# Mixer constants and gate rows loaded from GpSimd's queue, paired copies, and a split last product bank in a decoder layer

## The chip, the cores and the metric

The kernel runs on one core of a Trainium2 chip. The metric is the time of one execution in device microseconds. A core has five engines with instruction streams of their own, each of which runs its stream in order: TensorE (PE; the loading of its weights is listed apart as PEld), VectorE (DVE), ScalarE (ACT), GpSimd (POOL) and SyncE (SP). An engine that issues a transfer does so in its own stream; such issues are listed as SPq, ACTq or POOLq. Sixteen DMA engines carry the transfers of all queues.

## The reference

A decoder layer over 256 rows of width 1024: a half-weighted SwiGLU block, a token mixer, a second SwiGLU block, and a final RMSNorm. Each block is normalised, shifted, scaled and gated by vectors worked out from a conditioning row c.

```python
mod = (silu(c) @ w_ada + b_ada)                      # nine vectors of 1024
n = rmsnorm(h, g_ffn1) * (1 + sc1) + sh1
h = h + 0.5 * gt1 * ((silu(n @ w1_gate) * (n @ w1_up)) @ w1_down)
n = rmsnorm(h, g_mix) * (1 + sc2) + sh2
u, q, k, v = split(n @ w_in)                         # 512 columns each
y_pool = per group g of 4: ((mean over the last 2/4/8/16 rows) - u) @ w_pool[g] * pool_scale
y_attn = 8 heads of 64: three dilated causal windows with distance penalties, merged by their sums
h = h + gt2 * (concat(y_pool, y_attn) @ w_out)
n = rmsnorm(h, g_ffn2) * (1 + sc3) + sh3
h = h + 0.5 * gt3 * ((silu(n @ w2_gate) * (n @ w2_up)) @ w2_down)
out = rmsnorm(h, g_final)
```

The inner width of the SwiGLU blocks is 2816, cut into 11 chunks of 256. The three dilated windows are folded into one table of penalties (`bias`), 256 columns for each head, and the trailing means into band matrices (`band`), one for each of the four groups.

## The kernel before

The 256 rows are two tiles of 128, t = 0 and 1. All weights come through one sequence of units (`plan`), 1 MB each, which SyncE loads into four buffers `raw`. A unit of weights is split on the chip into a high part (`hi`, a cast on ScalarE, L288) and a low part (`lo`, a subtraction on VectorE, L289), and each product is done as three: hi by hi, low of the activations by hi, hi by low of the weights. A unit of the modulation (`ada`) is instead reduced on VectorE (L277). The order of the work within an engine is set by the Tile layer's scheduler, from the order of the code and from priorities (`urgent`).

`norm_rows` closes a block for one tile: gate (L330), add to h (L332), the sum of squares in two halves of 512 columns (L334), the power -0.5 on GpSimd (L337), and the scaled rows `xs` (L339 on ScalarE, L340 on VectorE). `norm_mod` turns them by TensorE (L316; `xt`, as `xtb` ahead of the mixer and `xtc` behind it) and applies shift and scale. The turns of tile 0 stand among the products of tile 1 of the same block (`accf`, `accm`), and those of tile 1 among the first products of the next block (`zp`, `le`).

In the mixer, `zchunk` makes the products `zp` and copies them to `z`; the turned `q` and `k` (`tq`, `tk`) come from it. `scores` multiplies them for a pair of heads, adds a bias table and exponentiates, `heads_out` turns the probabilities (`pt` to `pts`) and multiplies with v (`yt`), and `pool_group` does the band product (`po`) and the group's map (`pw`). Both write the mixer's output `y` as high and low part. All the constants of the mixer, the gate rows (`gate_rows`: through a small buffer `gd` in DRAM, then spread over 128 partitions into `gt`) and `gfb` are loaded from ScalarE's stream.

A load takes one of a few semaphores in turn, and so waits for the load that used it before. The loads of SyncE and ScalarE share one set of them (`DMAHW`); those of GpSimd have another (`DMASW`).

`finish3` ends the kernel: gate, add, sum of squares, scaling by the power and by `gfb`, and the store, in column parts. Ahead of it the last four chunks of tile 1 are multiplied for columns 0 to 511 first (`banks` (0,)), and then for 512 to 1023.

Of the kernel before, what the change touches and what calls it, by code (L numbers as in the profile page):

```python
# [10 lines left out]
F32 = mybir.dt.float32  # L11
# [4 lines left out]
P = 128  # L16
S = 256
# [28 lines left out]
SPIN = (4, 8, 8, 5)  # L46
PARTS = 11
# [123 lines left out]
def block_kernel(ctx, tc, w, vec, x, c, gf, wpool, bandd, biasd, out):  # L171
# [153 lines left out]
    def norm_rows(t, tag, accs, g, units):  # L325

        ss = None
        for b in range(2):
            tmp = work.tile([P, 512], F32, name=f"res{tag}{b}", tag="t2", bufs=T2)
            nc.vector.tensor_tensor(tmp, accs[b], g[:, ts(b, 512)], ALU.mult)  # L330
            hs = h[:, t * D + b * 512:t * D + b * 512 + 512]
            nc.vector.tensor_tensor(hs, hs, tmp, ALU.add)  # L332
            v = tiny.tile([P, 1], F32, name=f"v{tag}{b}", tag="v")
            nc.vector.tensor_tensor_reduce(tmp, hs, hs, 1.0, D * EPS if ss is None else ss, ALU.mult, ALU.add, v)  # L334
            ss = v
        r = tiny.tile([P, 1], F32, name=f"r{tag}", tag="r")
        nc.gpsimd.tensor_tensor(r, ss, mhalf, ALU.pow)  # L337
        xs = [work.tile([P, 512], F32, name=f"xs{tag}{b}", tag="t2", bufs=T2) for b in range(2)]
        rows = [nc.scalar.activation(xs[0], h[:, t * D:t * D + 512], AF.Copy, scale=r),  # L339
                nc.vector.tensor_scalar(xs[1], h[:, t * D + 512:t * D + D], r, None, ALU.mult)]  # L340
# [31 lines left out]
    def gate_rows(gtm, factor):  # L372
# [7 lines left out]
        nc.scalar.dma_start(d, sb)  # L380
        g = work.tile([P, D], F32, name=f"gt{gtm}", tag="gt", bufs=1)
        nc.scalar.dma_start(g, d.rearrange("(o a) b -> o (a b)", o=1).to_broadcast([P, D]))
# [38 lines left out]
    def down(f, ci, t, hid, accs, banks=(0, 1)):  # L421
        hi, lo = want("down", (f, ci))
        hh, hl = hid
        for k in range(2):
            first, last = ci == 0 and k == 0, ci == NCH - 1 and k == 1
            for (a, ww, st, sp) in ((hh, hi, first, False), (hl, hi, False, False), (hh, lo, False, last)):
                for b in banks:
                    mm(accs[b], a[:, k, :], cols(ww, 2 * k + b), start=st, stop=sp)  # L428

# [40 lines left out]
    def ffn_rest(f, ci0, n, prev, pci, accs, finish, gate):  # L470
# [19 lines left out]
        for banks in ((0, 1),) if f == 0 else ((0,), (1,)):  # L490
            for ci in last:
                if after and ci == last[TURN]:
                    after()
                down(f, ci, 1, hid[ci][1], accs[1], banks)
# [170 lines left out]
    probs = {}  # L665

    def scores(hp):
# [6 lines left out]
        both = xp.tile([P, 2 * S], F32, name=f"bias{hp}", tag="bias", bufs=3)  # L674
        nc.scalar.dma_start(both, biasd[:, 2 * hp * S:2 * hp * S + 2 * S])
        for e in range(2):
            hd = 2 * hp + e
            with urgent():
                ps, bias = pss[e], both[:, ts(e, S)]
# [4 lines left out]
                for t, sl in ((0, slice(0, P)), (1, slice(P, 3 * P))):  # L684
                    nc.vector.tensor_tensor_reduce(p[:, sl], ps[:, sl], bias[:, P:S] if t == 0 else bias, 1.0, 3e38,
# [8 lines left out]
    def heads_out(hp, v, y):  # L694
# [13 lines left out]
        with urgent():  # L708
            for t in range(NT):
                split(y[t][0][:, 4 + hp, :], y[t][1][:, 4 + hp, :], ps[:, ts(t, P)])  # L710

    def pool_group(g, u, y):
        bands = xp.tile([P, 2 * P + 16], F32, name=f"bands{g}", tag="bands", bufs=4)
        nc.scalar.dma_start(bands, bandd[:, g])
        wp = xp.tile([P, P], F32, name=f"wp{g}", tag="wp", bufs=4)
        nc.scalar.dma_start(wp, wpool[:, ts(g, P)])
# [101 lines left out]
    nc.scalar.dma_start(gfb, gf.to_broadcast([P, D]))  # L818
    nc.scalar.mul(gfb, gfb, float(D) ** 0.5)

    def finish3(t):
        with urgent():
# [3 lines left out]
            for part in (((0, 512),), ((512, 768), (768, D))):  # L826
                acc_b = nm["acc"][t][part[0][0] // 512]
                for a, b in part:
                    nc.vector.tensor_tensor(o[:, a:b], acc_b[:, a % 512:(b - 1) % 512 + 1], g[:, a:b], ALU.mult)
                for a, b in part:  # L830
                    nc.vector.tensor_tensor(ht[:, a:b], ht[:, a:b], o[:, a:b], ALU.add)
                for a, b in part:
                    sq = work.tile([P, 512], F32, name=f"sqo{t}{a}", tag="t2", bufs=T2)
                    n = (0, 512, 768).index(a)
                    nc.scalar.activation(sq[:, 0:b - a], ht[:, a:b], AF.Square, accum_out=ss[:, n:n + 1])
                    if n == 0:
                        nc.gpsimd.tensor_tensor(ss[:, 0:1], ss[:, 0:1], deps, ALU.add)
                for a, b in part:
                    nc.vector.tensor_tensor(o[:, a:b], ht[:, a:b], gfb[:, a:b], ALU.mult)
            v = tiny.tile([P, 1], F32, name=f"vo{t}", tag="v")  # L840
            nc.vector.tensor_scalar(v, ss[:, 1:2], ss[:, 2:3], ss[:, 0:1], ALU.add, ALU.add)
            r = tiny.tile([P, 1], F32, name=f"ro{t}", tag="r")
            nc.gpsimd.tensor_tensor(r, v, mhalf, ALU.pow)
            for a, b in ((0, 320), (320, 640)):
# [45 lines left out]
```

## Time and profile before

| | |
|---|---|
| Runs | 489.19, 489.13, 488.82 us (median 489.13) |
| Profiled execution | 489.54 us, span 487.6 us |
| Granted clock of TensorE, mean | 0.995 of full |
| Moved from and to DRAM | 126.05 MB, mean 259 GB/s |

The span is the time from the first to the last instruction that the profiler recorded; the rest of the execution's time lies around it. A group's row reads: line, engine, operation, output <- inputs, shapes, count. In a timeline a row begins with the start and the duration in us, and a bracket gives the time for which the engine had been idle and what ended that. A row of waits gives the total time, how often, and the longest. A window's row gives its length, the busy time of each engine with its number of instructions, the granted clock, the busy share of the DMA engines and GB/s. The chain of waits is followed back from the last instruction. A matmul's row is longer than the distance to the next, since matmuls overlap.

### The profile page before, as it was taken

The page shows a single profiled execution, that of the slowest core. Times are in us where ns is not written, and L with a number is a line of the kernel's source. Part 1 is how long each engine was busy: PE and PEld are TensorE (multiplying, and loading weights), DVE is VectorE, ACT ScalarE, POOL GpSimd, SP SyncE. Part 2 cuts the span into 40 slices and gives each one's busy share as a digit, 9 for nine tenths or more (in the row PEclk, how much of TensorE's full clock was granted, in tenths as well). Part 3 has the DMA queues.
Part 4 walks back from the last instruction along what each step waited for, and adds up shares of the span by engine and source line. Part 5 has one row for each costly group of instructions (what it writes and reads, how often), then busy time and mean ns, then how long its engine had stood idle before and what let it go on. Part 6 is the DMA issues. An engine that isn't in the chain of part 4 may idle for free.

```text
span 487.6 us, 5997 instructions
## 1 busy us (share of the span) xinstructions
PE 473.3 (97%) x2176; PEld 381.8 (78%) x2176; DVE 358.7 (74%) x587; ACT 259.0 (53%) x443; POOL 5.9 (1%) x18
## 2 busy tenths in 40 slices
PE   8999999999999999998989999999999999999994
PEld 5778888888888887787768777888878888888883
DVE  4978899996897874797899769965666756655244
ACT  3686585544554351893776477756443543544121
POOL 1000000000000000000000000000000000000000
PEclk9999999999999999999999999999999999999998
DMA  8999995997988890459977854996367758530002
GB/s 303 402 354 334 356 360 196 367 419 291 397 323 308 327 376 24 196 198 378 389 297 295 308 190 149 329 369 245 112 240 249 269 180 332 200 149 29 17 1 86
DMA packets 20383, 126.05 MB, mean 259 GB/s; under 512 B 2409, under 2 KB 4225, under 8 KB 6018
## 3 DMA queue, kind: packets, MB, share of 16 engines
q1 hardware_dynamic: 17568, 121.25, 65.8%
q10 hardware_dynamic: 2786, 4.43, 2.5%
q8 instruction: 17, 0.28, 0.2%
q14 instruction: 12, 0.10, 0.0%
HBM read 124.61 MB, written 1.06 MB: 258 GB/s over the span
## 4 chain that ended last, share of the span: by engine, by line
PE 83%; DMA 7%; DVE 4%; ACT 2%; issue 2%; POOL 1%; POOLq 0%; DVEq 0%; SPq 0%; ACTq 0%
PE accf L428 21%; PE gu L387 9%; PE gu L389 9%; PE gu L388 9%; PE ld L462 8%; PE le L462 8%; DMA raw<-in_w_dram 4%; PE accm L777 4%; DMA bands<-in_band_dram 2%; PE ht L414 2%; PE zp L389 2%; PE zp L387 2%; PE zp L388 2%; PE yt L707 1%; DVE h L332 1%
## 5 line engine op out<-in xcount | busy, mean ns | idle before, releaser
L289 DVE TENSOR_TENSOR lo<-raw,hi 128x1024 fp32r<-128x1024 f32 (+1 forms) x156 | 184.0, 1206 | 45.6 <-ACT hi L288 37.7
L288 ACT CAST hi<-raw 128x1024 fp32r<-128x1024 f32 (+1 forms) x156 | 158.6, 1046 | 77.0 <-DMA raw<-in_w_dram 32.8
L277 DVE CUSTOM_DVE_ANT_0 raw<-raw,cb,vecs 128x1024 f32<-128x1024 f32 x70 | 88.2, 1278 | 3.6 <-DMA raw<-in_w_dram 3.5
L428 PE MATMUL accf<-hi,hh 128*128 128x512 f32 x176 | 56.0, 394 | 0.2
L428 PE MATMUL accf<-hi,hl 128*128 128x512 f32 x176 | 55.7, 390 | 0.0
L428 PE MATMUL accf<-lo,hh 128*128 128x512 f32 x176 | 55.6, 390 | 0.0
L387 PE MATMUL gu<-hi,nhc 128*128 128x512 f32 x112 | 44.4, 396 | 0.0
L389 PE MATMUL gu<-lo,nhc 128*128 128x512 f32 x112 | 43.7, 390 | 0.0
L388 PE MATMUL gu<-hi,nlc 128*128 128x512 f32 x112 | 43.6, 389 | 0.0
L405 ACT ACTIVATE sg<-gu 128x256 f32<-128x256 f32 x24 | 9.2, 382 | 64.2 <-PE gu L389 64.2
L428 PEld LDWEIGHTS accf<-hi,hl 128*128 128x128 f32 x176 | 32.8, 188 | 7.4 <-DVE hl L309 0.7
L428 PEld LDWEIGHTS accf<-lo,hh 128*128 128x128 f32 x176 | 33.0, 188 | 7.0
L428 PEld LDWEIGHTS accf<-hi,hh 128*128 128x128 f32 x176 | 32.4, 188 | 7.2 <-ACT hh L308 1.1
L408 DVE TENSOR_TENSOR pr<-sg,gu 128x256 f32<-128x256 f32 x24 | 10.0, 418 | 32.3 <-ACT sg L405 32.3
L387 PE MATMUL gu<-hi,nha 128*128 128x512 f32 x80 | 31.7, 396 | 0.0
L389 PE MATMUL gu<-lo,nha 128*128 128x512 f32 x80 | 31.2, 390 | 0.0
L388 PE MATMUL gu<-hi,nla 128*128 128x512 f32 x80 | 31.1, 389 | 0.0
L309 DVE TENSOR_TENSOR hl<-ht,hh 128x256 fp32r<-128x256 f32 x44 | 16.4, 416 | 14.4 <-ACT hh L308 14.4
L308 ACT CAST hh<-ht 128x256 fp32r<-128x256 f32 x44 | 14.1, 379 | 23.0 <-PE ht L414 23.0
L387 PE MATMUL zp<-hi,nhb 128*128 128x512 f32 x64 | 26.1, 411 | 0.0
L389 PE MATMUL zp<-lo,nhb 128*128 128x512 f32 x64 | 25.2, 394 | 0.0
L388 PE MATMUL zp<-hi,nlb 128*128 128x512 f32 x64 | 25.1, 392 | 0.0
(167 smaller groups left out, 709.3 us busy)
## 6 DMA issues: line engine op xcount, KB each, us to landing
raw<-in_w_dram SPq DMA_DIRECT2D x112, 1024.0 KB, 5.8
raw<-in_w_dram SPq DMA_DIRECT2D x4, 512.0 KB, 7.6
gt<-gd ACTq DMA_DIRECT2D x3, 512.0 KB, 5.0
h<-in_x_dram SPq DMA_DIRECT2D x2, 512.0 KB
bias<-in_bias_dram ACTq DMA_DIRECT2D x4, 256.0 KB, 7.5
out_dram<-o SPq DMA_DIRECT2D x4, 160.0 KB, 2.1
bands<-in_band_dram ACTq DMA_DIRECT2D x4, 136.0 KB, 8.1
gfb<-in_gf_dram ACTq DMA_DIRECT2D x1, 512.0 KB, 5.3
```

The lines of the kernel that those rows point to most:

```text
L277: note(nc.vector.tensor_tensor_reduce(r, r, cb, 1.0, vecs[:, m:m + 1], ALU.mult, ALU.add, mod[:, m:m + 1]), i, 1)
L288: note(nc.scalar.copy(hi[:, o:o + n], src), i + s / 2, 0)
L289: note(nc.vector.tensor_tensor(lo[:, o:o + n], src, hi[:, o:o + n].bitcast(F32), ALU.subtract), i + s / 2, 0)
L308: nc.scalar.copy(hi_ap, src)
L309: nc.vector.tensor_tensor(lo_ap, src, hi_ap.bitcast(F32), ALU.subtract)
L387: mm(ps, nh[:, k, :], whi, start=first, stop=False)
L388: mm(ps, nl[:, k, :], whi, start=False, stop=False)
L389: mm(ps, nh[:, k, :], wlo, start=False, stop=last)
L408: nc.vector.tensor_tensor(pr, sg, ps[:, 256:512], ALU.mult)
L428: mm(accs[b], a[:, k, :], cols(ww, 2 * k + b), start=st, stop=sp)
L462: mm(banks[ci][t], n[t][a][:, j, :], cols(ww, lead_set(f, j).index(ci)), start=j == 0 and p == 0, stop=last and p == 2)
L777: mm(acc2[t][b], a[:, k, :], cols(ww, 2 * kk + b), start=st, stop=sp)
```

## The change

Four edits in one. Mixer constants: the four bias loads become two (`bias0` in the mixer's memory, `bias1` in the buffer of the gate row), the four loads each of bands and wp become one each, and all of these, the gate rows and `gfb` are issued by GpSimd. `norm_rows`: the first half's sum of squares is a Square on ScalarE, to which GpSimd adds the epsilon, and VectorE's second half starts from that. Mixer copies: for both tiles first the two high copies, then the two low subtractions. The end: for chunks 9 and 10 the products of tile 1's last 512 columns are done as two halves of 256, the second into a bank of its own (`far`), and `finish3` is rewritten to match.

```diff
+SPLIT = (9, 10)
 def norm_rows(t, tag, accs, g, units):
-            nc.vector.tensor_tensor_reduce(tmp, hs, hs, 1.0, D * EPS if ss is None else ss, ALU.mult, ALU.add, v)
+            if b == 0:
+                nc.scalar.activation(tmp, hs, AF.Square, accum_out=v)
+                nc.gpsimd.tensor_tensor(v, v, deps, ALU.add)
+            else:
+                nc.vector.tensor_tensor_reduce(tmp, hs, hs, 1.0, ss, ALU.mult, ALU.add, v)
 def gate_rows(gtm, factor):
-        nc.scalar.dma_start(d, sb)
+        nc.gpsimd.dma_start(d, sb)
-        nc.scalar.dma_start(g, d.rearrange("(o a) b -> o (a b)", o=1).to_broadcast([P, D]))
+        nc.gpsimd.dma_start(g, d.rearrange("(o a) b -> o (a b)", o=1).to_broadcast([P, D]))
+    def down_halves(f, chunks, hid, acc_b, other):
+        for c0, ps in ((0, acc_b), (256, other)):
+            n = 0
+            for ci in chunks:
+                hi, lo = want("down", (f, ci))
+                for k in range(2):
+                    for a, ww in ((hid[ci][0], hi), (hid[ci][1], hi), (hid[ci][0], lo)):
+                        n += 1
+                        mm(ps[:, 0:256], a[:, k, :], cols(ww, 2 * k + 1)[:, c0:c0 + 256], start=c0 > 0 and n == 1,
+                           stop=n == 6 * len(chunks))
 def ffn_rest(f, ci0, n, prev, pci, accs, finish, gate):
-                down(f, ci, 1, hid[ci][1], accs[1], banks)
+                if f == 0 or banks == (0,) or ci < SPLIT[0]:
+                    down(f, ci, 1, hid[ci][1], accs[1], banks)
+        if f == 1:
+            nm["far"] = psp.tile([P, 256], F32, name="far", tag="ps")
+            down_halves(f, SPLIT, {ci: hid[ci][1] for ci in SPLIT}, accs[1][1], nm["far"])
+    bias = [xp.tile([P, 4 * S], F32, name="bias0")]
+    band_all = xp.tile([P, 4, 2 * P + 16], F32, name="band_all")
+    wp_all = xp.tile([P, 4 * P], F32, name="wp_all")
+    nc.gpsimd.dma_start(bias[0], biasd[:, 0:4 * S])
 def scores(hp):
-        both = xp.tile([P, 2 * S], F32, name=f"bias{hp}", tag="bias", bufs=3)
-        nc.scalar.dma_start(both, biasd[:, 2 * hp * S:2 * hp * S + 2 * S])
+        both = bias[hp // 2][:, ts(hp % 2, 2 * S)]
 def heads_out(hp, v, y):
             for t in range(NT):
-                split(y[t][0][:, 4 + hp, :], y[t][1][:, 4 + hp, :], ps[:, ts(t, P)])
+                nc.scalar.copy(y[t][0][:, 4 + hp, :], ps[:, ts(t, P)])
+            for t in range(NT):
+                nc.vector.tensor_tensor(y[t][1][:, 4 + hp, :], ps[:, ts(t, P)], y[t][0][:, 4 + hp, :].bitcast(F32),
+                                        ALU.subtract)
 def pool_group(g, u, y):
-        bands = xp.tile([P, 2 * P + 16], F32, name=f"bands{g}", tag="bands", bufs=4)
-        nc.scalar.dma_start(bands, bandd[:, g])
-        wp = xp.tile([P, P], F32, name=f"wp{g}", tag="wp", bufs=4)
-        nc.scalar.dma_start(wp, wpool[:, ts(g, P)])
+        bands, wp = band_all[:, g], wp_all[:, ts(g, P)]
...
     after = finish1(1)
+    bias.append(work.tile([P, 4 * S], F32, name="bias1", tag="gt", bufs=1))
+    nc.gpsimd.dma_start(bias[1], biasd[:, 4 * S:8 * S])
+    nc.gpsimd.dma_start(band_all, bandd)
+    nc.gpsimd.dma_start(wp_all, wpool)
...
-    nc.scalar.dma_start(gfb, gf.to_broadcast([P, D]))
+    nc.gpsimd.dma_start(gfb, gf.to_broadcast([P, D]))
 def finish3(t):
-            for part in (((0, 512),), ((512, 768), (768, D))):
...
+            add(nm["acc"][t][0], 0, 512)
+            square(0, 0, 512, deps)
+            add(nm["acc"][t][1], 512, D)
+            square(1, 512, 768, ss[:, 0:1])
+            if t:
+                add(nm["far"], 768, D)
+            nc.vector.tensor_tensor_reduce(o[:, 768:D], ht[:, 768:D], ht[:, 768:D], 1.0, ss[:, 1:2], ALU.mult, ALU.add,
+                                           ss[:, 2:3])
             r = tiny.tile([P, 1], F32, name=f"ro{t}", tag="r")
-            nc.gpsimd.tensor_tensor(r, v, mhalf, ALU.pow)
-            for a, b in ((0, 320), (320, 640)):
+            nc.gpsimd.tensor_tensor(r, ss[:, 2:3], mhalf, ALU.pow)
+            nc.vector.tensor_tensor(o[:, 768:D], ht[:, 768:D], gfb[:, 768:D], ALU.mult)
+            for a, b in ((0, 192), (192, 640)):
```

Here `add` is the gate and the add to h on VectorE, and `square` is a Square on ScalarE, an add of its sum on GpSimd and the product with `gfb` on VectorE.

Three places show what moves. The first is SyncE's queue in the mixer: the same eight weight units, `raw`, with the semaphores that each load waits for (`DMAHW` are loads, `DVE` is VectorE). Before:

```order
L272 DMA raw_1895<-in_w_dram 128x2048 [waits DMAHW0_49,DVE_49]
L272 DMA raw_1899<-in_w_dram 128x2048 [waits DMAHW2_49,DVE_49]
L272 DMA raw_1924<-in_w_dram 128x2048 [waits DMAHW1_49,DVE_49]
L272 DMA raw_1928<-in_w_dram 128x2048 [waits DMAHW5_49,DVE_49]
L272 DMA raw_1984<-in_w_dram 128x2048 [waits DMAHW3_49,DVE_49]
L272 DMA raw_1988<-in_w_dram 128x2048 [waits DMAHW6_49,DMAHW1_49,DVE_49]
L272 DMA raw_2085<-in_w_dram 128x2048 [waits DMAHW7_49,DMAHW5_49,DVE_49]
L272 DMA raw_2089<-in_w_dram 128x2048 [waits DMAHW6_49,DMAHW0_49,DVE_49]
```

And after:

```order
L273 DMA raw_1905<-in_w_dram 128x2048 [waits DMAHW6_49,DVE_49]
L273 DMA raw_1909<-in_w_dram 128x2048 [waits DMAHW0_49,DVE_49]
L273 DMA raw_1934<-in_w_dram 128x2048 [waits DMAHW2_49,DVE_49]
L273 DMA raw_1938<-in_w_dram 128x2048 [waits DMAHW7_49,DVE_49]
L273 DMA raw_1994<-in_w_dram 128x2048 [waits DMAHW1_49,DVE_49]
L273 DMA raw_1998<-in_w_dram 128x2048 [waits DMAHW3_49,DVE_49]
L273 DMA raw_2095<-in_w_dram 128x2048 [waits DMAHW4_49,DVE_49]
L273 DMA raw_2099<-in_w_dram 128x2048 [waits DMAHW5_49,DVE_49]
```

The order of the loads is the same; three of them waited for two other loads and now wait for one.

The second is GpSimd's stream from the end of the first block to the mixer (`vb`, `rb`: sum and power of a norm's tile; `gd`, `gt`: a gate row). Before, from the norm of the input (`rx`) to the norms behind the mixer (`rc`), nothing else stood in it:

```order
L534 TENSOR_TENSOR rx_151<-vx_149,mhalf 128x1
L534 TENSOR_TENSOR rx_170<-vx_168,mhalf 128x1
L337 TENSOR_TENSOR rb_1754<-vb_1752,mhalf 128x1
L337 TENSOR_TENSOR rb_1858<-vb_1856,mhalf 128x1
L337 TENSOR_TENSOR rc_2654<-vc_2652,mhalf 128x1
L337 TENSOR_TENSOR rc_2742<-vc_2740,mhalf 128x1
```

After, the part from the first gate row to the second:

```order
L385 DMA gd_1541<-gs_1539 8x128
L387 DMA gt_1543<-gd_1541 128x1024
L337 TENSOR_TENSOR vb_1747<-vb_1747,deps 128x1
L342 TENSOR_TENSOR rb_1755<-vb_1753,mhalf 128x1
L690 DMA bias_1849<-in_bias_dram 128x1024
L760 DMA bias_1870<-in_bias_dram 128x1024
L337 TENSOR_TENSOR vb_1856<-vb_1856,deps 128x1
L761 DMA band_all<-in_band_dram 128x1088
L342 TENSOR_TENSOR rb_1864<-vb_1862,mhalf 128x1
L762 DMA wp_all<-in_wpool_dram 128x512
L385 DMA gd_2435<-gs_2433 8x128
L387 DMA gt_2437<-gd_2435 128x1024
```

Where two powers followed each other (`rb`), there now stand between them two bias loads, an add and the bands load.

The third is TensorE in the mixer's output product (`accm`) at the turns of tile 0's rows (`xtc`). Before:

```order
L777 MATMUL accm_2536<-hi_1_2095,nhy_1866 128x512
L777 MATMUL accm_2537<-hi_1_2095,nhy_1866 128x512
L777 MATMUL accm_2536<-hi_1_2095,nly_1867 128x512
L316 MATMUL xtc_2698<-ident,xsc_2656 128x128 x4
L316 MATMUL xtc_2714<-ident,xsc_2657 128x128 x4
L777 MATMUL accm_2537<-hi_1_2095,nly_1867 128x512
```

After:

```order
L805 MATMUL accm_2522<-hi_1_2105,nhy_1876 128x512
L317 MATMUL xtc_2685<-ident,xsc_2643 128x128 x4
L317 MATMUL xtc_2701<-ident,xsc_2644 128x128 x4
L805 MATMUL accm_2523<-hi_1_2105,nhy_1876 128x512
L805 MATMUL accm_2522<-hi_1_2105,nly_1877 128x512
L805 MATMUL accm_2523<-hi_1_2105,nly_1877 128x512
```

The turns stand two products earlier; so do those of tile 0 ahead of the mixer and of tile 1 behind it, while those of tile 1 ahead of the mixer stand three products later.

More of the change, by code (lines that the diff above doesn't have):

```diff
@@ L678, in scores @@
             with urgent():
-                ps, bias = pss[e], both[:, ts(e, S)]
+                ps, off = pss[e], both[:, ts(e, S)]
                 p = xp.tile([P, 384], F32, name=f"p{hd}", tag="p", bufs=4)
@@ L684, in scores @@
                 for t, sl in ((0, slice(0, P)), (1, slice(P, 3 * P))):
-                    nc.vector.tensor_tensor_reduce(p[:, sl], ps[:, sl], bias[:, P:S] if t == 0 else bias, 1.0, 3e38,
+                    nc.vector.tensor_tensor_reduce(p[:, sl], ps[:, sl], off[:, P:S] if t == 0 else off, 1.0, 3e38,
                                                    ALU.add, ALU.min, mx[:, t:t + 1])
@@ L728, in pool_group @@
             for t in range(NT):
-                yh, yl = y[t]
-                nc.scalar.activation(yh[:, g, :], p2[:, ts(t, P)], AF.Copy, scale=sc)
-                nc.vector.scalar_tensor_tensor(yl[:, g, :], p2[:, ts(t, P)], sc, yh[:, g, :].bitcast(F32),
+                nc.scalar.activation(y[t][0][:, g, :], p2[:, ts(t, P)], AF.Copy, scale=sc)
+            for t in range(NT):
+                nc.vector.scalar_tensor_tensor(y[t][1][:, g, :], p2[:, ts(t, P)], sc, y[t][0][:, g, :].bitcast(F32),
                                                ALU.mult, ALU.subtract)
     after = finish1(1)
+    bias.append(work.tile([P, 4 * S], F32, name="bias1", tag="gt", bufs=1))
+    nc.gpsimd.dma_start(bias[1], biasd[:, 4 * S:8 * S])
+    nc.gpsimd.dma_start(band_all, bandd)
+    nc.gpsimd.dma_start(wp_all, wpool)
     QS = -DH ** -0.5
@@ L825, in finish3 @@
             ht, g = h[:, ts(t, D)], nm["g3"]
-            for part in (((0, 512),), ((512, 768), (768, D))):
[L827 to L839, printed above, removed]
@@ L840, in finish3, with add, square @@
-            v = tiny.tile([P, 1], F32, name=f"vo{t}", tag="v")
-            nc.vector.tensor_scalar(v, ss[:, 1:2], ss[:, 2:3], ss[:, 0:1], ALU.add, ALU.add)
+            def add(src, a, b):
+                nc.vector.tensor_tensor(o[:, a:b], src, g[:, a:b], ALU.mult)
+                nc.vector.tensor_tensor(ht[:, a:b], ht[:, a:b], o[:, a:b], ALU.add)
+            def square(n, a, b, more):
+                sq = work.tile([P, 512], F32, name=f"sqo{t}{a}", tag="t2", bufs=T2)
+                nc.scalar.activation(sq[:, 0:b - a], ht[:, a:b], AF.Square, accum_out=ss[:, n:n + 1])
+                nc.gpsimd.tensor_tensor(ss[:, n:n + 1], ss[:, n:n + 1], more, ALU.add)
+                nc.vector.tensor_tensor(o[:, a:b], ht[:, a:b], gfb[:, a:b], ALU.mult)
```

## The prediction

> **What bounds the kernel now.** I read the page's engine shares first, then who waits for whom on TensorE, then stretches around the edits, then the mixer's chain.
>
> ```profile
> PE 473.3 (97%) x2176; PEld 381.8 (78%) x2176; DVE 358.7 (74%) x587; ACT 259.0 (53%) x443; POOL 5.9 (1%) x18
> ```
> ```profile
> PE yt L707 <- ACT pts L702: 1.5, 1, 1.5
> ...
> PE tk L316 <- ACT z L660: 1.3, 1, 1.3
> PE xtc L316 <- ACT xsc L339: 0.9, 2, 0.4
> ...
> PE xtb L316 <- ACT xsb L339: 0.8, 2, 0.6
> ```
> ```profile
> 196.00:214.00 18.00, 17.74 (x85) 14.44 (x84) 15.99 (x26) 16.78 (x39) 0.57 (x1) 1.00 0.49 191
> 214.00:246.00 32.00, 29.20 (x147) 22.63 (x145) 26.75 (x56) 21.42 (x41) 0.00 (x0) 1.00 0.95 359
> ```
>
> TensorE is busy for 473.3 of 487.6 us, so whatever this change brings has to come out of 14.3 us of gaps (or add to them). Half of that, 7.2 us, is the end, where TensorE has finished (its last product ends at 480.4, which the last fence of the tail shows). Inside, the second fence gives 2.8 us to the mixer (yt 1.5, tk 1.3) and 1.7 us to the four places where normalised rows are turned (xtb 0.6 and 0.2, xtc twice 0.45). The change touches all three groups and nothing else that TensorE waits for. The windows show why the mixer waits: from 214 to 246 the DMA engines are 95% busy, while the stretch just ahead, 196 to 214, has them at 49%.
>
> ```profile
> SPq L272 <- DMA bias<-in_bias_dram: 6.6, 1, 6.6
> SPq L272 <- DVE lo L289: 4.9, 2, 3.1
> ```
> ```profile
> 220.95 0.93 ACTq L714 DMA_DIRECT2D bands<-in_band_dram  x1
> ...
> 227.25 1.99 ACT L288 CAST hi<-raw 128x1024 fp32r<-128x1024 f32 x2 [3.61 <-DMA raw<-in_w_dram]
> 229.16 0.59 ACT L660 ACTIVATE z<-zp 128x512 f32<-128x512 f32 x1
> ```
> ```profile
> 223.06 8.12 DMA bands<-in_band_dram
> ...
> 243.18 0.94 ACT hi L288
> 244.11 0.49 ACT z L660
> ...
> 245.02 1.02 PE yt L707 x5
> ```
>
> In that crowded stretch the small constants do damage twice. A weight load on SyncE's queue stood 6.6 us for a bias load (first fence). ScalarE issues those constants from its own instruction stream, 0.93 us for the one shown, and the z that tk needed came only at 229.16, behind two casts whose weights were 3.61 us late. The chain passes through a bands load for 8.12 us and ends at yt.
>
> **The mixer's constants (gain).**
>
> ```profile
> L685 DVE CUSTOM_DVE_ANT_0 p<-sc,bias x16: 278/356/420, 233.4 to 256.7; 128x128 f32<-128x128 f32 x8, 128x256 f32<-128x256 f32 x8
> ```
>
> Twelve loads leave ScalarE's stream (bias x4, bands x4, wp x4) and become four on GpSimd's queue: bias0 and bias1 just after the first norms, then all bands and all wp. Their 512 + 512 + 544 + 256 KB, 1.8 MB, now come in the 196 to 214 stretch, where some 9 us of 18 are free on the DMA engines. SyncE no longer shares a wait with them, since the after order shows one load wait where there were two. Their first reader is the scores' reduction at 233.4 by this row, some 25 us later, and the band products follow later still, so their own lateness is covered. All but the first bias load (256 KB) leave the crowded stretch: 1.5 MB at its 359 GB/s, about 4 us of transfer, which exceeds both waits. In the new order z also stands ahead of the second cast. So tk's 1.3 us goes. What is late next is yt: behind it ScalarE still does a cast, a z and the first pts one after the other, 0.93 + 0.49 + 0.42 = 1.84 us by the chain rows, 243.18 to 245.02, from z's input, now with z first; TensorE has six transposes and four zp products in that time, about 1.5 us (0.11 and 0.227 each, below). I leave it 0.45 us of the 1.5 us and, as TensorE arrives there 1.3 us sooner and ScalarE may not have caught up, another 0.25 us: 0.8 gained. Mixer: -1.3 - 0.8 = -2.1 us, bounded by -2.8 (both waits gone) and -1.0 (only most of the first). The paired copies (both hi copies, then both lo subtractions) are the same number of instructions and only reorder two engines whose waits here are those counted; I cost them at 0, hidden by the zp and accm products that fill TensorE.
>
> **The first sum of squares on ScalarE (loss).** In each of four norms one reduction of 512 columns leaves VectorE; a ScalarE Square and a GpSimd add take its place, and VectorE's second reduction waits for that add.
>
> ```profile
> 190.76 1.28 DVE L332 TENSOR_TENSOR h<-h,resb 128x512 f32<-128x512 f32 x2
> ...
> 192.80 0.75 DVE L334 CUSTOM_DVE_ANT_0 resb<-h,vb 128x512 f32<-128x512 f32 x1
> ```
> ```profile
> 471.39 0.63 ACT L835 ACTIVATE sqo<-h 128x512 f32<-128x512 f32 x1 [4.29 <-DVE h L831]
> 471.93 0.18 ACT L835 ACTIVATION_READ_ACCUMULATOR sqo<-h 128x1 f32 x1
> ```
> ```profile
> 472.19 0.48 POOL L837 TENSOR_TENSOR sso<-sso,deps 128x1 f32<-128x1 f32 x1 [174.94 <-ACT sqo L835]
> ...
> 477.52 0.19 POOL L837 TENSOR_TENSOR sso<-sso,deps 128x1 f32<-128x1 f32 x1 [2.94 <-ACT sqo L835]
> 482.88 0.55 POOL L843 TENSOR_TENSOR ro<-vo,mhalf 128x1 f32<-128x1 f32 x1 [5.17 <-DVE vo L841]
> ```
>
> The first half of h is done at 190.76 + 0.64 = 191.40. Square with its accumulator read takes 0.72 (471.39 to 472.11), the hop to GpSimd 0.08, the add 0.19 to 0.48, the hop back some 0.05: 192.45 to 192.75, against 192.80 now. I take 0.19, the row in which VectorE was idle, as it will be here: the chain is 0.3 us shorter (0.05 to 0.35). But the new order puts the turns two products earlier (0.227 each, below) in three of the four norms, so TensorE arrives 0.45 us sooner for rows that come 0.3 us sooner: +0.15 us each, +0.45 (0.3 to 1.2) in all.
>
> The fourth place is the second norm ahead of the mixer, where the turns stand three products later instead.
>
> ```profile
> 201.65 1.29 DVE L330 TENSOR_TENSOR resb<-accf,gt 128x512 f32<-128x512 f32 x2 [0.56 <-PE accf L428]
> ```
> ```profile
> 203.24 1.13 ACT L288 CAST hi<-raw 128x1024 fp32r<-128x1024 f32 x1
> ```
> ```profile
> 205.93 0.57 POOL L337 TENSOR_TENSOR rb<-vb,mhalf 128x1 f32<-128x1 f32 x1 [11.68 <-DVE vb L334]
> ```
> ```profile
> 207.31 1.09 PE L316 MATMUL xtb<-ident,xsb 128*128 128x128 f32 x8 [0.26 <-ACT xsb L339]
> ```
>
> Square comes after one cast: 204.37 + 0.72 = 205.09; the add ends at 205.36 to 205.65, the reduction 0.83 later at 206.2 to 206.5, and the power some 0.15 behind it. From the power's start to the turns it is 207.31 - 205.93 = 1.38 us, so 207.75 to 208.05; TensorE is there at 207.05 + 0.68 = 207.73. Wait 0 to 0.3 against 0.26: -0.1.
>
> On GpSimd, though, the bias1 load (which waits for VectorE's last read of the gate row, at 201.65 + 1.29, as it takes that buffer) now stands ahead of this add, and the bands load between the add and the power. No row shows what a load costs GpSimd to issue. ScalarE's quickest shown here bounds it from below,
>
> ```profile
> 263.56 0.30 ACTq L380 DMA_DIRECT2D gd<-gs  x1
> ```
>
> 0.30; from above I take its slowest, the 0.93 of 220.95, times 2.5, the ratio of the two GpSimd adds (0.48 beside a busy VectorE, 0.19 beside an idle one): 2.3 us. I take 0.93, since the bands load is that transfer. With an issue cost c, bias1 is free up to c = 2.2 (202.9 to 205.17) and bands up to c = 1.0 (the reduction covers it); above both the turns are late by 2c - 3.2. At 0.93 it costs 0, at 2.3 it costs 1.4 us. The page "DMA: Bandwidth & Descriptors" of the Trainium skill (Latency and other measured facts) puts the emission overhead of a GpSimd load near 1 us; by that estimate the sum stays as it is, and no run here shows it yet.
>
> **Gate rows and gfb (0).** The three gate rows go through GpSimd too, each two issues, the second waiting for the first to land.
>
> ```profile
> gt<-gd ACTq DMA_DIRECT2D x3, 512.0 KB, 5.0
> ```
> ```profile
> 280.33 1.06 ACT L819 ACTIVATE gfb<-gfb 128x1024 f32<-128x1024 f32 x1 [4.46 <-DMA gfb<-in_gf_dram]
> ```
>
> The tightest is the middle one, ready at 263.5 and read when the norm behind the mixer begins, about when gfb is multiplied (280.3): with as much as 5 us of landing for either transfer and 2c of 4.6 at most, 2 us are left. The gfb load moves ahead of where it is now, and ScalarE waits there 4.46 us already.
>
> **The last products (gain).** Twelve products of 512 columns become twelve of 256 into the old bank and twelve of 256 into a new one.
>
> ```profile
> 458.04 8.16 PE accf L428 x36
> 466.20 0.44 PE ht L414 x4
> ```
> ```profile
> 475.93 0.69 DVE L831 TENSOR_TENSOR h<-h,o 128x512 f32<-128x512 f32 x1
> 476.66 0.69 DVE L839 TENSOR_TENSOR o<-h,gfb 128x512 f32<-128x512 f32 x1
> 480.39 0.76 DVE L829 TENSOR_TENSOR o<-accf,gt 128x256 f32<-128x256 f32 x2 [3.04 <-PE accf L428]
> ```
>
> A 512-column product takes 8.16/36 = 0.227; a 128-column transpose with its own weight load 0.11. So 256 columns lie between 0.11 and 0.148 (interpolated); half of 0.227 is 0.114, I take 0.12: 24 x 0.12 = 2.88 against 2.72, +0.16. The first twelve end at 480.36 - 2.72 + 1.44 = 479.08; VectorE then does 512-wide multiply and add (0.73 from start to start) and a 256-wide gfb product (0.38), until 480.93, later than the far bank at 480.5. From there multiply 0.44, add 0.44, reduction about 0.45 and a hop of 0.1: the power starts at 482.4 against 482.88. Gain 0.5 (0.15 to 0.65). The small add vo is gone from that path. The last store grows from 320 to 448 columns, for which I take off 0.1: tail -0.4 (-0.55 to 0).
>
> Sum: -2.1 + 0.45 - 0.1 - 0.4 = -2.15 us. The profiled execution took 489.54 (span 487.6, 1.9 around it), 0.41 above the median of the runs, so it would take 487.4, and the median 489.13 - 2.15 = 487.0.
>
> **Rivals.**
> 1. GpSimd's issues are slow because VectorE keeps it out (slower). The fence of windows has VectorE busy 15.99 of 18 us from 196 to 214, and the 0.48 against 0.19 us add shows that it can stretch GpSimd's work. At c = 3.1 the turns come 2c - 3.2 = 3.0 us late and the sum is +0.85: 490.0; the gain is gone from c = 2.7 on. Against it: the read that stretched was by two-input VectorE work, and VectorE waits during part of this stretch. "SBUF — State Buffer" of the Trainium skill (SBUF: two separate sides) has this as a trap: a load from GpSimd took about 620 ns alone and 3100 ns beside a VectorE copy, because its descriptors could not be written. It also holds that two-input VectorE work takes only the shared read side; no row here decides.
> 2. The weights stay late (no change). SyncE also stood for VectorE's lo (4.9 us) in that stretch; if that paces the casts, the mixer's 2.8 us only move. Left are +0.35 and -0.4: 489.1. For it: VectorE is busy 26.75 of 32 us there. Against: VectorE's gaps there end with late weights, and the chain runs through bands, not lo.
> 3. ScalarE catches up fully (faster): both mixer waits go, the far bank gives its 0.65, the norms cost nothing: -3.4, 485.7.
>
> **Numbers.** The forecast 0.58, rival 1 0.14, rival 2 0.17, rival 3 0.11. The likeliest alone spans 486.0 to 488.6 by the bounds of its terms. The range 485.7 to 489.2 leaves out rival 1 and a little of the others. A measurement of this kernel tells about 0.2% (1 us) from nothing: faster 0.66 (forecast nearly whole, rival 3), same 0.22 (rival 2 and the milder half of rival 1), slower 0.12.
>
> **What would show it.** Right: no bias, bands or wp among SyncE's waits; tk's wait gone and yt's under 0.8; GpSimd's loads near 1 us; turn waits of 0.7 and under 0.3 ahead of the mixer and 0.6 twice behind it; the power at the end 1.9 us after the last product (2.5 now). Wrong: a GpSimd load of over 2 us around 203 to 207 with xtb waiting for it, far products over 0.15 us each, or yt still waiting 1.5 us.

## The result, and the profile after

The changed kernel takes 485.73 us (median of 4 runs, 485.44 to 485.93); the kernel before, run beside it, 489.16. The ratio is 0.9929 (95% interval 0.9912 to 0.9947): 3.4 us faster, where the forecast was 2.15 us. The profiled execution took 485.93 us, span 484.1. A second measurement of the same kernel (e13) gave 485.59, ratio 0.9915.

The page's engine shares, and then all that TensorE waits for (total, times, longest):

```profile
PE 472.5 (98%) x2188; PEld 382.6 (79%) x2188; DVE 357.8 (74%) x579; ACT 261.7 (54%) x447; POOL 14.9 (3%) x35
```
```profile
PE xtc L317 <- ACT xsc L344: 1.4, 2, 0.7
PE spin L523 <- POOL ident masks.py:199: 1.4, 1, 1.4
PE xt L317 <- ACT xs L526: 0.8, 1, 0.8
PE xtb L317 <- ACT xsb L344: 0.7, 1, 0.7
```

Both mixer waits, tk and yt, are gone entirely; the turn waits behind the mixer have grown from 0.45 to 0.7 each. The same two stretches as before the change, with engine busy times, clock, DMA share and GB/s at the end:

```profile
196.00:214.00 18.00, 18.00 (x88) 14.87 (x87) 15.09 (x22) 16.80 (x39) 2.48 (x5) 1.00 0.77 276
214.00:246.00 32.00, 32.00 (x164) 24.75 (x163) 30.11 (x68) 24.75 (x47) 0.00 (x0) 1.00 0.84 332
```

TensorE is busy for all of the 32 us in which it was busy for 29.20, and the DMA engines have gone from 0.49 and 0.95 to 0.77 and 0.84: traffic has moved from the crowded stretch into the one ahead of it.

Busy time alone would mislead, since TensorE's total fell by only 0.8 us. A product's row lasts 0.39 us while the next starts 0.23 us behind it, so the first 0.16 us of every stall lies inside a busy row. Two places that both programs have, the second turn of q and the transpose for the gate row (`gp`), give the mixer from start to start; first before, then after (timeline: start, duration):

```profile
222.42 0.60 PE L316 MATMUL tq<-ident,z 128*128 128x128 f32 x4
...
260.81 0.27 PE L376 MATMUL gp<-ident,mod 128*8 128x128 f32 x1
```
```profile
222.58 0.60 PE L317 MATMUL tq<-ident,z 128*128 128x128 f32 x4
...
257.33 0.27 PE L381 MATMUL gp<-ident,mod 128*8 128x128 f32 x1
```

That is 38.39 against 34.75 us: 3.64 us gone, where the waits recorded there were 2.8. Matched row by row, 1.45 us of it lie ahead of tk, 1.70 around the first yt and 0.44 around the second yt, where no wait is listed.

The edges of the program, after: GpSimd's loads with their issue times, and the tail.

```profile
203.85 0.54 POOL L760 DMA_DIRECT2D bias<-in_bias_dram  x1 [8.81 <-DVE resb L331]
205.29 0.19 POOL L337 TENSOR_TENSOR vb<-vb,deps 128x1 f32<-128x1 f32 x1 [0.91 <-ACT resb L336]
205.75 0.56 POOL L761 DMA_DIRECT2D band_all<-in_band_dram  x1 [0.27 <-issue]
206.37 0.56 POOL L342 TENSOR_TENSOR rb<-vb,mhalf 128x1 f32<-128x1 f32 x1
206.89 0.68 POOL L762 DMA_DIRECT2D wp_all<-in_wpool_dram  x1
```
```profile
478.95 0.08 DVE L871 DVE_READ_ACCUMULATOR2_ANT sso<- 128x1 f32 x1
479.07 0.43 DVE L875 TENSOR_TENSOR o<-h,gfb 128x256 f32<-128x256 f32 x1
479.11 0.79 POOL L874 TENSOR_TENSOR ro<-sso,mhalf 128x1 f32<-128x1 f32 x1 [1.09 <-DVE sso L871]
479.94 0.61 ACT L879 ACTIVATE o<-o,ro 128x384 f32<-128x384 f32 x1 [2.25 <-POOL ro L874]
```

A load costs GpSimd 0.54 to 0.68 us here, and the power of the second norm starts 0.06 us after the bands' issue ends, with no visible loss. At the end the power starts early, as meant, but lasts 0.79 us.

### The profile page after: what moved, and what is told of

Same layout as the page of the kernel before. It is cut to its first block, busy times and chain, and to the rows that moved or that the text cites. A ratio compares the mean times of both kernels' runs of the same rounds, so it can differ in the third digit from the quotient of the medians.

```text
span 484.1 us, 6040 instructions
## 1 busy us (share of the span) xinstructions
PE 472.5 (98%) x2188; PEld 382.6 (79%) x2188; DVE 357.8 (74%) x579; ACT 261.7 (54%) x447; POOL 14.9 (3%) x35
## 4 chain that ended last, share of the span: by engine, by line
PE 91%; DVE 3%; ACT 2%; issue 1%; DMA 1%; POOL 1%; POOLq 0%; DVEq 0%; ACTq 0%
PE accf L433 23%; PE gu L394 9%; PE gu L392 9%; PE gu L393 9%; PE le L479 8%; PE ld L479 8%; PE accm L805 4%; PE zp L392 3%; PE zp L394 3%; PE zp L393 3%; PE ht L419 2%; PE yt L731 1%; DMA h<-in_x_dram 1%; PE sh L394 1%; PE ld L394 1%
## 5 line engine op out<-in xcount | busy, mean ns | idle before, releaser
L278 DVE CUSTOM_DVE_ANT_0 raw<-raw,cb,vecs 128x1024 f32<-128x1024 f32 x70 | 88.2, 1280 | 1.2 <-DMA raw<-in_w_dram 1.2
L433 PE MATMUL accf<-hi,hh 128*128 128x512 f32 x172 | 54.5, 394 | 0.2
L433 PE MATMUL accf<-hi,hl 128*128 128x512 f32 x172 | 54.4, 391 | 0.0
L433 PE MATMUL accf<-lo,hh 128*128 128x512 f32 x172 | 53.9, 389 | 0.0
```

Of the source, the lines that this page charges most:

```text
L278: note(nc.vector.tensor_tensor_reduce(r, r, cb, 1.0, vecs[:, m:m + 1], ALU.mult, ALU.add, mod[:, m:m + 1]), i, 1)
```

## The experiments

**The constants alone (e1).** On the kernel before, only the twelve loads become four on GpSimd's queue.

```diff
+    nc.gpsimd.dma_start(bias[0], biasd[:, 0:4 * S])      # ahead of scores
+    nc.gpsimd.dma_start(bias[1], biasd[:, 4 * S:8 * S])  # these three behind finish1(1)
+    nc.gpsimd.dma_start(band_all, bandd)
+    nc.gpsimd.dma_start(wp_all, wpool)
-        nc.scalar.dma_start(both, ...); nc.scalar.dma_start(bands, ...); nc.scalar.dma_start(wp, ...)
```

> The kernel before with one part of the change alone: the mixer's constants in four transfers from GpSimd's queue. Theory (weights on time): both mixer stalls and their hidden parts go, which the two traces put at 1.48 for tk, 1.6 and 0.3 for the first two yt and some 0.4 in the pool stage, so about -3.5 us: 485.6 (485.0 to 486.2), with no yt or tk among TensorE's waits over 0.3 us. Rival (the forecast's size was right for this part, the rest came from elsewhere): -2.1, 487.0, with yt still waiting 0.7 us.

Measured: 485.26 us, ratio 0.9907 (0.9884 to 0.9929), no tk and no yt among TensorE's waits. This part alone brings 4.1 us, more than the whole change.

**Where the gain comes from: the queue or the time (e2, e6).** Two kernels with the same four transfers as the changed one. In e2 ScalarE issues them:

```diff
-    nc.gpsimd.dma_start(bias[1], biasd[:, 4 * S:8 * S])   # and so for all four
+    nc.scalar.dma_start(bias[1], biasd[:, 4 * S:8 * S])
```

> The changed kernel with the same four transfers of constants, at the same places in the code, issued by ScalarE instead of GpSimd. Theory A (few and early is what counts): same as the changed kernel within 0.5 us, 485.7 (485.3 to 486.3). Rival B (the queue counts: on ScalarE they share the set of semaphores with the weights and hold ScalarE's stream at the wait for the gate row's buffer): a bias, bands or wp load comes back among SyncE's waits with over 1 us, and the time is 487 or more.

In e6 GpSimd issues them, but three of them must wait for a value of k0:

```diff
+    for c in (bias[1][:, 0:1], band_all[:, 0, 0:1], wp_all[:, 0:1]):
+        nc.gpsimd.tensor_tensor(c, z["k0"][:, 0:1], deps, ALU.add)
     nc.gpsimd.dma_start(bias[1], biasd[:, 4 * S:8 * S])   # and the bands, and wp
```

> The changed kernel with three of the four transfers (bias1, the bands, wp: 1.3 MB) held on GpSimd's queue until z of k0 is there, about 215 instead of 204 to 207. Theory (the time of the transfer counts): the weights are late again as from ScalarE, with a tk wait over 1 us, 487.5 to 489.4. Rival (the queue counts: no shared semaphore with the weights, nothing in ScalarE's stream): 485.7 within 0.5.

Measured: e2 489.39 (ratio 0.9993, 0.998 to 1.0007), e6 489.54 (1.0015, 0.9997 to 1.0032). Both lose everything. ScalarE's last three issues in e2 (timeline, start and duration):

```profile
214.32 0.33 ACTq L760 DMA_DIRECT2D bias<-in_bias_dram  x1
216.80 0.33 ACTq L761 DMA_DIRECT2D band_all<-in_band_dram  x1
220.22 0.33 ACTq L762 DMA_DIRECT2D wp_all<-in_wpool_dram  x1
```

In its stream the loads stand behind the norm's shifts and casts and come 10 to 13 us later than from GpSimd. But e2 is no clean test of that, since its scheduler also put a reduction of the modulation (L278) ahead of five lo subtractions on VectorE, where the changed kernel has the five first:

```profile
225.44 1.28 DVE L278 CUSTOM_DVE_ANT_0 raw<-raw,cb,vecs 128x1024 f32<-128x1024 f32 x1 [6.89 <-DMA raw<-in_w_dram]
226.65 5.76 DVE L290 TENSOR_TENSOR lo<-raw,hi 128x1024 fp32r<-128x1024 f32 x5
```

VectorE stood 6.89 us for the late unit of that reduction. SyncE, which waits for buffers that VectorE frees, issued no weight between 218.58 and 229.03, and from 228 to 232 the DMA engines were busy for only 0.39 of the time.

In e6 GpSimd issues them at 219.2 to 220.3; below are its rows, then rows of the DMA view (KB, us from issue to landing), of TensorE's waits, and of the chain of waits:

```profile
219.21 0.59 POOL L775 DMA_DIRECT2D bias<-in_bias_dram  x1
...
220.32 0.54 POOL L777 DMA_DIRECT2D wp_all<-in_wpool_dram  x1
```
```profile
band_all<-in_band_dram POOLq DMA_DIRECT2D x1, 544.0 KB, 13.1
wp_all<-in_wpool_dram POOLq DMA_DIRECT2D x1, 256.0 KB, 14.6
```
```profile
PE yt L731 <- ACT pts L726: 2.2, 1, 2.2
```
```profile
222.66 11.45 DMA raw<-in_w_dram
234.11 0.02 issue
234.13 2.00 ACT hi L289 x2
```

In the chain, a weight load issued at 222.66 takes 11.45 us beside them, and from its cast the chain runs to yt. The tk wait that was expected of e6 is only 0.2 us. In neither kernel does a bias, bands or wp load appear among SyncE's waits. So the shared wait on SyncE that the forecast read as one of two kinds of damage is not needed for the loss: in e6 the transfers are late on GpSimd's own queue, and the gain is gone; early on it (e1, and most of it in e5 below), the gain stays. The scheduler reorders parts of the mixer in both kernels, so that time and order change together; the next runs say how far. An early issue from ScalarE or SyncE was not tried, so GpSimd is shown to be early here, not to be the only way.

**How much of it (e9, e10).** The same hold as in e6, for bias1 alone (0.5 MB), and for the bands and wp alone (0.8 MB).

> The changed kernel with only bias1 (0.5 MB) held on GpSimd's queue until z of k0 is there. Holding all three transfers (1.3 MB) cost about 4 us. Theory A (each late byte costs TensorE the same, since the weights behind it come later by its transfer): 0.5/1.3 of 4, +1.6, 487.2 (486.6 to 487.8). Theory B (there is slack for some of it, and only what exceeds it stalls): under +0.6, 485.7 to 486.3.

> The changed kernel with only the bands and wp (0.8 MB) held on GpSimd's queue until z of k0 is there. Theory A (each late byte costs the same): +2.5, 488.1 (487.4 to 488.8). Theory B (slack first): 486.0 to 487.4, less than 0.8/1.3 of what all three cost.

Measured: 487.69 (ratio 0.9967, 0.9954 to 0.998) and 487.78 (0.9969, 0.9954 to 0.9983), each about 2 us above the changed kernel. Both show a tk wait again (1.0 and 0.55 us). Two parts of 2.0 and 2.1 make the 3.9 of e6 (all against 485.66, the middle of the changed kernel's two medians), so there is no slack that swallows the first half megabyte; in proportion to bytes they are not, since 0.8 MB cost no more than 0.5. The loss lies in the mixer: from the second turn of q to gp it takes 36.71 us in e9, 36.40 in e10 and 38.00 in e6, against 34.75 in the changed kernel and 34.76 in e1.

Not all of this is late weights. In the kernel before and in e5, e6, e9 and e10, ScalarE makes two casts ahead of the z that tk needs; in the changed kernel, e1 and e12 (the last kernel below) it makes one. First e9, where tk waits 0.98 us, then e12:

```profile
226.88 1.99 ACT L289 CAST hi<-raw 128x1024 fp32r<-128x1024 f32 x2 [3.30 <-DMA raw<-in_w_dram]
228.78 0.59 ACT L681 ACTIVATE z<-zp 128x512 f32<-128x512 f32 x1
```
```profile
226.51 1.05 ACT L289 CAST hi<-raw 128x1024 fp32r<-128x1024 f32 x1 [3.48 <-DMA raw<-in_w_dram]
227.46 0.59 ACT L677 ACTIVATE z<-zp 128x512 f32<-128x512 f32 x1
```

In e12 this cast starts 4.71 us behind the second turn of q, about as late as before the change (4.83), and tk waits 0.21 us instead of 1.32. So about a microsecond at tk is the scheduler's order, which changes along with the loads and which no run holds fixed. The first yt goes with the weights: where the third cast behind that turn starts 11.4 us (e6) or 11.8 us (before) behind it, yt waits 2.17 and 1.48 us; where it starts 7.7 to 10.2 us behind it (the changed kernel, e1, e5, e9 to e12), at most 0.14. Some order is in this too: between pt and yt stands one zp product in e6, three before the change, and four in the changed kernel.

**Few or many (e5).** The kernel before, its twelve loads as they were, from GpSimd.

```diff
-        nc.scalar.dma_start(both, biasd[:, 2 * hp * S:2 * hp * S + 2 * S])   # so bands and wp
+        nc.gpsimd.dma_start(both, biasd[:, 2 * hp * S:2 * hp * S + 2 * S])
```

> The kernel before with its twelve loads of mixer constants kept as they are, but issued by GpSimd, where they stand right behind the norms' powers. Theory (out of ScalarE's stream they come early, ahead of the crowded stretch, whatever their number): as with the four transfers alone, 485.3 (485.0 to 486.0). Rival (few large transfers count, since each GpSimd issue of 0.55 us delays the second norm's power): 486.5 or more, with xtb waiting 1 us or more.

Measured: 486.16, ratio 0.9939 (0.9916 to 0.9963). Eleven of the twelve are issued by 208.4; the fourth bias needs a buffer that VectorE frees at 233.7, where its 256 KB take 6.9 us to land in the crowded stretch. tk waits 0.15 again. Most of the gain needs no merging. The last 0.9 us, by the medians, stay open: the intervals of e1 and e5 overlap, and e5 has, besides that late load, both casts ahead of z.

**The Square undone (e3).** The four norms go back to two reductions on VectorE; the rest is the changed kernel.

```diff
-            if b == 0:
-                nc.scalar.activation(tmp, hs, AF.Square, accum_out=v)
-                nc.gpsimd.tensor_tensor(v, v, deps, ALU.add)
-            else:
-                nc.vector.tensor_tensor_reduce(tmp, hs, hs, 1.0, ss, ALU.mult, ALU.add, v)
+            nc.vector.tensor_tensor_reduce(tmp, hs, hs, 1.0, D * EPS if ss is None else ss, ALU.mult, ALU.add, v)
```

> The changed kernel with the first half's sum of squares back on VectorE in the four norms. Theory (Square brings the rows sooner by less than the turns were moved forward): the four turn waits, 2.64 us in start-to-start terms after against 2.35 before, fall by 0.3 and the time to 485.4 (485.0 to 485.7). Rival (freeing VectorE of four 0.75 us reductions helped the lows ahead of the mixer): 486.0 to 486.6, with a wait for lo or z back on TensorE.

Measured: 485.08, ratio 0.9903 (0.9882 to 0.9924). TensorE's waits at the turns:

```profile
PE xtc L317 <- ACT xsc L340: 0.9, 2, 0.5
...
PE xtb L317 <- ACT xsb L340: 0.5, 1, 0.5
```

They sum to 1.4 against 2.1 with the Square, and the time falls by 0.65 by the medians. The intervals of the two kernels overlap, so it is the waits that carry this: the Square costs about 0.7 us. The second xtb, 0.26 before, waits for nothing with or without it.

**The pairing undone (e4).**

```diff
-                nc.scalar.copy(y[t][0][:, 4 + hp, :], ps[:, ts(t, P)])     # both tiles, then both lows
+                split(y[t][0][:, 4 + hp, :], y[t][1][:, 4 + hp, :], ps[:, ts(t, P)])   # so in pool_group
```

> The changed kernel with the mixer's output copies back in the order high, low, high, low. Theory (the pairing costs and brings nothing, as forecast): 485.7 within 0.3. Rival (the pairing is where the extra gain over the forecast came from, in the pool stage): 486.1 to 486.7, with the pool stage longer by 0.4 us or more.

Measured: 485.67, ratio 0.9918 (0.9896 to 0.994): nothing, as forecast.

**The end (e7, e8).** e7 has the end of before, with no halves and the old `finish3`. e8 keeps the halves and moves the products with gfb behind the power:

```diff
-            nc.vector.tensor_tensor(o[:, 768:D], ht[:, 768:D], gfb[:, 768:D], ALU.mult)
-            for a, b in ((0, 192), (192, 640)):
-                nc.vector.tensor_scalar(o[:, a:b], o[:, a:b], r, None, ALU.mult)
+            for a, b in ((512, 768), (768, D)):
+                nc.vector.scalar_tensor_tensor(o[:, a:b], ht[:, a:b], r, gfb[:, a:b], ALU.mult, ALU.mult)
...
-            nc.scalar.activation(o[:, 640:D], o[:, 640:D], AF.Copy, scale=r)
+            nc.scalar.activation(o[:, 0:512], o[:, 0:512], AF.Copy, scale=r)
```

> The changed kernel with the end of before: no halves, the old order of the last tile. By the two traces the new end starts the power 0.39 us sooner but the power takes 0.24 us longer beside VectorE's product, so 0.13 us are lost by undoing it: 485.9 (485.6 to 486.2). By the forecast's term, 0.4 lost: 486.1.

> The changed kernel with the products of the last 512 columns with gfb taken from ahead of and beside the power and done behind it, together with the scaling by the power, in one operation of VectorE (two of 256 columns), while ScalarE scales columns 0 to 511. Theory (VectorE's product beside it stretches the power): the power takes 0.55 us again instead of 0.79 and starts 0.34 us sooner, so -0.5: 485.2 (485.0 to 485.5). Rival (the power is slow there for another reason, or the store ends later): 485.6 or more.

Measured: e7 485.83 (0.9931, 0.9909 to 0.9954), e8 485.63 (0.9929, 0.9906 to 0.9953). Neither differs from the changed kernel by what can be told apart. In e8 the power is short again and starts 1.73 us after the last product (1.99 in the changed kernel):

```profile
478.58 0.55 POOL L876 TENSOR_TENSOR ro<-sso,mhalf 128x1 f32<-128x1 f32 x1 [0.67 <-DVE sso L873]
479.16 0.72 ACT L880 ACTIVATE o<-o,ro 128x512 f32<-128x512 f32 x1 [1.74 <-POOL ro L876]
479.16 0.88 DVE L878 SCALAR_TENSOR_TENSOR o<-h,ro,gfb 128x256 f32<-128x256 f32 x2 [0.66 <-POOL ro L876]
```

The cause of the long power is shown, and the half microsecond is not got: from the power's end to the end of the span it takes 4.6 us instead of 4.2, since VectorE's work behind the power (0.88) is longer than it was (0.68) and the last stores leave later against it.

**The gate rows (e11, e13 to e16).** e11 and e14 are the changed kernel with the gate rows and gfb on ScalarE again, e13 the changed kernel itself beside e14, e15 that edit alone on the kernel before, e16 that edit with the constants.

> The changed kernel with the gate rows and gfb issued by ScalarE again. Forecast and theory (two us of cover on either queue): same as the changed kernel, 485.7 within 0.4. Rival (their place in GpSimd's stream is what delays the norms, or ScalarE's issues hold its stream): 0.5 or more to either side, with a turn's wait changed by as much.

> The changed kernel itself, beside the next three on one chip. If its time depends on how quickly the weights land around 217 to 232 (5.0 us for the first of them in its profile, 7.5 in that of the kernel with the gate rows on ScalarE), it can come out up to 1 us above 485.7 with a tk wait of some 0.5 us; else 485.7 within 0.3.

> The kernel with the gate rows and gfb on ScalarE once more. Theory (the 1.5 us above the changed kernel came from slower landings in that run, which the gate rows have no part in, 40 us away from them): within 0.5 us of the changed kernel beside it. Rival (the queue of the gate rows is worth it): again 1.2 to 2 us above the changed kernel.

> The kernel before with the gate rows and gfb on GpSimd's queue alone. Theory (worth nothing): 489.1 within 0.5. Rival: 487.2 to 488.0.

> The kernel before with the mixer's constants and the gate rows and gfb on GpSimd's queue, and nothing else. Theory (the gate rows are worth nothing): as with the constants alone, 485.3 within 0.5. Rival: 483.6 to 484.2.

Measured: e11 487.40 (0.9957, 0.9945 to 0.9969), e13 485.59 (0.9915, 0.9894 to 0.9936), e14 486.64 (0.9939, 0.9917 to 0.996), e15 488.88 (0.9983, 0.9969 to 0.9998), e16 484.77 (0.9896, 0.987 to 0.9922). Undoing the edit costs 1.7 us (e11) and 1.0 (e14), which is not nothing; adding it alone brings 0.4 (e15, inside the range of "worth nothing"), and to the constants 0.5 (e16, just outside). By the medians these two are at the limit of what the runs resolve, but the traces agree: from gp to the first turn behind the mixer it takes 24.78 us before and 24.43 in e15, 24.66 in e1 and 24.21 in e16, 24.18 in the changed kernel, and 24.88 and 25.76 in e11 and e14. ScalarE's timeline of e14, in an execution of 487.73 us, 1.1 above its median, shows where the largest of these comes from:

```profile
267.27 0.37 ACT L747 COPY pl<-po 128x256 f32<-128x256 f32 x1
269.29 1.05 ACT L289 CAST hi<-raw 128x1024 fp32r<-128x1024 f32 x1 [1.65 <-DMA raw<-in_w_dram]
270.25 0.62 ACT L753 ACTIVATE nhy<-pw,vecs 128x128 fp32r<-128x128 f32 x2
270.76 0.86 ACT L726 COPY pts<-pt 128x384 f32<-128x384 f32 x2
```
```profile
PE yt L731 <- ACT pts L726: 1.3, 1, 1.3
```

With the gate row's issues in ScalarE's stream, the scheduler puts a weight's cast ahead of the last pool copies and of pts; in the changed kernel it stands behind pts. Its weight is 1.65 us late, and the last yt waits 1.3 us. Two things go into that, and no run separates them: the order of ScalarE's stream, and the gate row's transfer. In e14 that transfer is issued ahead of the weight (261.37 and 261.96) and lands in 4.1 us, and the weight reaches ScalarE 7.3 us after its issue; in the changed kernel the weight is issued first (261.62) and lands in 4.8 us, and the gate row takes 8.3. In e11 a yt wait of 0.4 and a tk wait of 0.8 share the loss; its weight for tk was issued at 217.3, as early as in e13, and landed in 7.5 us against 5.1 there and 5.0 in e14. Why was not settled.

**The two best parts together (e12).** The changed kernel with e3's norms and e8's end.

> The changed kernel with the four norms' reductions back on VectorE, and the last products with gfb done behind the power together with the scaling. Theory (the two add up): 0.65 and 0.1 below the changed kernel, 485.0 (484.6 to 485.3). Rival (the four turns' waits come back elsewhere when the rest shifts): 485.5 or more.

Measured: 484.82 (484.5 to 485.11), ratio 0.9908 (0.9895 to 0.992), below every run of the changed kernel. e16, constants and gate rows alone, is as fast.

## Why the prediction was wrong

- **The mixer's constants: right mechanism, half the size.** Forecast -2.1, measured -4.1 (e1). The step that failed is yt: 0.8 of its 1.5 us was to go, and all of it went. ScalarE's work between z's input and the first pts was put right, 1.84 us against about 1.85 in the rows below (z from 240.24, the first of two pts done about 242.1). TensorE's work in that time was put at 1.5 us, transposes and four zp products, and left out the three zp products between z's last product and the transposes:

```profile
239.75 0.39 PE L394 MATMUL zp<-lo,nhb 128*128 128x512 f32 x1
239.98 0.39 PE L392 MATMUL zp<-hi,nhb 128*128 128x512 f32 x1
240.20 0.39 PE L393 MATMUL zp<-hi,nlb 128*128 128x512 f32 x1
240.43 0.39 PE L394 MATMUL zp<-lo,nhb 128*128 128x512 f32 x1
240.66 0.81 PE L723 MATMUL pt<-ident,p 128*128 128x128 f32 x6
...
242.34 0.67 PE L731 MATMUL yt<-pts,z 128*64 128x256 f32 x2
```
```profile
240.24 0.60 ACT L681 ACTIVATE z<-zp 128x512 f32<-128x512 f32 x1 [0.48 <-PE zp L394]
240.73 1.04 ACT L289 CAST hi<-raw 128x1024 fp32r<-128x1024 f32 x1
241.67 0.86 ACT L726 COPY pts<-pt 128x384 f32<-128x384 f32 x2
```

  From the start of z's last product to yt it is 2.6 us, so the first pts is ready some 0.25 us before yt needs it, and ScalarE even waits for z's input (0.48). The 0.25 us taken off for a ScalarE that had not caught up was wrong too. The second miss is the bound: 2.8 us, both recorded waits, was taken as the most that could go, while from start to start the stretch lost 3.64. Rival 3 (both waits go) described the mixer, but that it also named the time, 485.7, is luck: it had 0.65 from the end, which gave about 0.1, and the norms for nothing, which cost about 0.7.
- **The Square: right sign, low.** Forecast +0.45 for three places: +0.65 by e3, and the three waits grew by 0.17, 0.27 and 0.26. The -0.1 for the fourth place belongs to the constants: e1 has no second xtb wait either.
- **GpSimd's issue cost: below what was taken, and free.** 0.54 to 0.68 us against 0.93. Rival 1 needed 2.7. The page "DMA: Bandwidth & Descriptors" of the Trainium skill (Latency and other measured facts) puts the first byte of a GpSimd load at about 1 us, as emission overhead; the rows here time the issue alone, and no run shows the first byte.
- **The tail: a term that did not come.** Forecast -0.4; undoing it cost 0.1 (e7), which is no measurable difference. The products were right (0.12 us each, 475.5 to 476.8 for the twelve into `far`), the power's start too (1.99 us after the last product, 1.9 forecast). The failed step is the power itself, which was carried on at 0.55 us and took 0.79 beside the product with gfb that the edit puts there; e7's and e8's power, without it, take 0.55.
- **Gate rows and gfb: forecast 0.** Some 0.4 to 0.5 by e15 and e16. The transfers' own landing was covered, as forecast; that two issues reorder ScalarE's stream, and that the gate row's transfer can go ahead of a weight, was left out.
- **Rival 2 (the weights stay late)** is out: e1 has no mixer wait.
- **The sum.** -4.1 constants, +0.65 Square, -0.45 gate rows, -0.1 end is -4.0, against -3.4 and -3.65 in the two measurements. Each term carries about 1 us of interval, so that is as well as they close. The stated 486.0 to 488.6 does not follow from the terms at its upper end, where their worst values add up to +0.1, 489.2; the measured time lies below its lower end, at the edge of the wider range.

## What to carry to other kernels

Ask of a small load not which queue it costs but in which stretch its bytes land: move it to a time when the DMA engines are half idle, from a stream that reaches it early, and look at the order that the scheduler makes of the rest. To size what can be had from a stall, measure from start to start on the waiting engine, and count all of the work that stands between the producer's input and the consumer, from the new order. Each edit that adds or removes an instruction lets the scheduler move its neighbours, so price the new order, and undo parts one by one: here one of four cost about 0.7 us of what another had won.

## What the runs showed of the hardware

- **GpSimd's arithmetic waits for VectorE, its load issues do not.** The power of the input's norm beside VectorE's reduction of the second tile. First the changed kernel's profile (its powers as shortest/median/longest in ns), then e13, the same kernel:

```profile
6.28 1.22 DVE L553 CUSTOM_DVE_ANT_0 xs<-h 128x1024 f32<-128x1024 f32 x1
```
```profile
L555 POOL TENSOR_TENSOR rx<-vx,mhalf x2: 543/1082/1621, 6.3 to 7.9; 128x1 f32<-128x1 f32 x2
```
```profile
6.34 1.23 DVE L553 CUSTOM_DVE_ANT_0 xs<-h 128x1024 f32<-128x1024 f32 x1 [0.22 <-DMA h<-in_x_dram]
...
6.27 0.55 POOL L555 TENSOR_TENSOR rx<-vx,mhalf 128x1 f32<-128x1 f32 x1 [4.93 <-DVE vx L553]
```

  Where VectorE had begun 0.02 us earlier (6.28 against 6.30), the first power took 1.62 us and ended 0.4 us after VectorE's operation; where GpSimd was 0.07 us ahead, it took 0.55. The power at the end, 0.79 us, also ends 0.4 us after VectorE's product. In e6 three adds of one column, beside VectorE's mod and lo work, took 0.78, 1.24 and 1.19 us, and the three load issues right behind them, beside the same lo work, 0.53 to 0.59; in all runs together an issue takes 0.53 to 0.73. The page "SBUF — State Buffer" of the Trainium skill (SBUF: two separate sides) describes a lock that GpSimd waits for until VectorE is done, also where VectorE has two inputs and the GpSimd operation reads SBUF. The powers and adds agree with it; the trap it names, a load from GpSimd held up beside a VectorE copy, no load issue of these runs shows.
- **The same weight load takes 5.0 to 7.5 us** from one run to another: 5.02 us in e14 (issued at 217.91) and 7.53 in e11 (at 217.32), which are one kernel with the same loads around it. In e14 tk does not wait, in e11 it waits 0.8 us.
